# Spreading c by matmuls at the head, and the last six products in column pieces at the tail

## The chip, the core and the metric

The kernel runs on one core of one Trainium2 chip. Five engines work side by side, each through its own list of instructions in a fixed order: TensorE (PE, matmuls), VectorE (DVE), ScalarE (ACT), GpSimd (POOL) and SyncE (SP), which issues all transfers. An engine that waits for another holds up everything behind it in its own list. The metric is the device time of one execution in microseconds; the time before is the median of three runs.

## The reference

One decoder block for 1024 positions of width 1024 in float32. All six shifts, scales and gates, and the two of the last norm, come from one vector c:

```python
c_act = jax.nn.silu(c)
cond = c_act @ ada_w[i] + ada_b[i]
shift1, scale1, gate1, shift2, scale2, gate2 = jnp.split(cond, N_MOD, axis=-1)
h = modulate(rmsnorm(x, norm1_g[i]), shift1, scale1)
z = h @ w_in[i] + b_in[i]
...
x = x + gate1[:, None, :] * (y @ w_out[i])
h2 = modulate(rmsnorm(x, norm2_g[i]), shift2, scale2)
g_ff, up_ff = jnp.split(h2 @ w_ffn_in[i], 2, axis=-1)
x = x + gate2[:, None, :] * ((jax.nn.silu(g_ff) * up_ff) @ w_ffn_out[i])
shift_f, scale_f = jnp.split(c_act @ ada_f_w + ada_f_b, 2, axis=-1)
return modulate(rmsnorm(x, norm_f_g), shift_f, scale_f)
```

Between `z` and `y` stand a spatial gating mixer and a convolution; the change touches neither.

## The kernel before

**Layout.** Activations are stored transposed: eight tiles x0 to x7 of 128 channels by 1024 positions, worked on in two halves of 512 positions. A product in float32 is made of three matmuls on rounded parts (high by high, low by high, high by low, `mm3`, L731 to L733). For this each weight and each activation is split: ScalarE rounds it to the high part, and VectorE or GpSimd subtracts to get the low part. One column of conditioning (128 channels of one of the eight vectors) is a product of c with 128 rows of `ada_w`: the rows are loaded as a tile of 128 by 1024, and VectorE multiplies this with `cact` (silu of c, the same row in all partitions) and sums along it (`ada_cols`, L687).

**The head.** SyncE loads c as one row (L639), the eight tiles of the first half of x (L645), the small columns (L647), and then for k = 0 to 7 the two conditioning columns scale and shift (into the four `ypad` buffers) and the weights `wk`. TensorE copies c to all partitions by a matmul with ones (L661), and ScalarE applies Silu to it. The sums of squares for the first norm are matmuls with ones into 32 rows each (`rstd`, L780; the squares have five buffers, so the sixth waits for the first of these groups); then come the root (L783), the reciprocal (L784) and a broadcast back to 128 partitions (L786), and ScalarE copies the result to `r1a` (L792). Fourteen matmuls on ones (L669) stand where the planner puts them. For each k the tile is multiplied by the norm (L861), rounded with scale and shift by ScalarE (L863), its low part is made (L864, L865), and 24 matmuls add it into eight banks.

**The tail.** The last FFN projection is done by seven products per pair of tiles and halves, as in Strassen's scheme; products 5 and 3 end in the second half of the positions. In its last round, for n = 0 to 3, each product goes through L1063 and is added to x by VectorE (L1413). The final norm is made in pieces: half 0, and two pieces of 256 positions (`pieces`). Squares come from ScalarE (L1340) and are added by GpSimd (L1345) or go one by one to the sums (`to_partitions`, L1332); `norm` makes root, reciprocal and broadcast (L1361 to L1364), `output` multiplies (VectorE L1380, or GpSimd L1376), shifts (ScalarE L1382, L1377) and stores each tile (L1383). Of the last products only (3, 3) is cut in two pieces, and both of its pieces' norms follow it.

**What sets the order.** The code records all instructions; at its end `fix_order` plans the order of each engine's list from a table of durations (`duration`, `Clock`) and pins it. `issue_after` adds an edge that keeps one instruction behind another on the same engine.

## Time and profile before

| | us |
|---|---|
| median of three runs | 984.29 (983.1 to 984.59) |
| the profiled execution | 982.54 |
| its span | 980.7 |
| TensorE busy | 962.7 |
| first product starts | 18.22 |
| last product ends | 964.4 |
| last store issued | 978.3 |

The profile is of one execution of its own, and its times are counted from the start of the span. TensorE's busy time holds overlapping ends of matmuls; what tells where the time goes is the chain of waits, followed back from the last instruction, and the timeline of a stretch. A line of the timeline holds start, length, engine, source line, operation, tiles, and in brackets the idle time ahead of it with what ended it.

### The profile page before, as it was taken

Reading aid. Unit: us, or ns where it says so; the run is one execution under the profiler, and the core shown is the slowest. Engines: PE = TensorE matmul, PEld = TensorE weight load, DVE = VectorE, ACT = ScalarE, POOL = GpSimd, SP = SyncE. Lnnn points to the kernel's source line nnn. Section 1 sums busy time; section 2 is a strip of 40 time slices with the busy share of each in tenths; the row PEclk is TensorE's granted clock in tenths of the full one; section 3 lists DMA queues with packets and bytes.
Section 4 is the critical chain, followed back from the end, with each engine's and each line's share of the span. In section 5 each row is a group of like instructions: output and inputs, shape, how many; then the busy total and the mean of one; then the engine's idle time right before and its main releaser. Section 6 shows DMA issues by size and latency. Waiting matters only on the chain.

```text
span 980.7 us, 13307 instructions
## 1 busy us (share of the span) xinstructions
PE 962.7 (98%) x4673; PEld 778.2 (79%) x4673; DVE 852.3 (87%) x1200; ACT 474.8 (48%) x748; POOL 393.7 (40%) x232
## 2 busy tenths in 40 slices
PE   9999999999999999999999999999999999999994
PEld 5888777788878778888888888888888888888873
DVE  5999989999999563899999999989979989879946
ACT  6788566733563652564333233333338337236416
POOL 0068888646454312663454444454542100000221
PEclk9999999999999999999999999999999999999997
DMA  8982442433565334864777667665659838224104
GB/s 329 337 321 75 153 170 83 154 108 135 161 230 183 134 104 163 279 213 140 250 237 255 220 229 257 239 225 187 250 188 320 287 111 266 97 67 149 33 1 172
DMA packets 73668, 184.10 MB, mean 188 GB/s; under 512 B 8193, under 2 KB 10497, under 8 KB 73602
## 3 DMA queue, kind: packets, MB, share of 16 engines
q1 hardware_dynamic: 73602, 183.25, 54.5%
q8 instruction: 37, 0.61, 0.2%
q14 instruction: 29, 0.24, 0.1%
HBM read 142.06 MB, written 41.16 MB: 187 GB/s over the span
## 4 chain that ended last, share of the span: by engine, by line
PE 93%; ACT 2%; DVE 2%; DMA 1%; issue 1%; SPq 0%; ACTq 0%; DVEq 0%
PE B L1063 30%; PE C L1063 18%; PE ah L1063 10%; PE A L1063 3%; PE po L733 3%; PE po L731 3%; PE po L732 3%; PE p L731 3%; PE p L732 3%; PE p L733 3%; PE v L733 2%; PE pu L731 2%; PE v L731 2%; PE pu L733 2%; PE v L732 1%; PE pu L732 1%
## 5 line engine op out<-in xcount | busy, mean ns | idle before, releaser
L1063 PE MATMUL B<-h,w_f 128*128 128x512 f32 x816 | 191.0, 389 | 0.1
L1063 PEld LDWEIGHTS B<-h,w_f 128*128 128x128 f32 x816 | 153.0, 188 | 32.4 <-DVE w_f L1056 0.7
L1001 DVE SCALAR_TENSOR_TENSOR cv<-ypad,colt,cv 128x512 f32<-128x512 f32 x216 | 147.7, 747 | 0.2
L1063 PE MATMUL B<-fa,w_d 128*128 128x512 f32 x528 | 125.6, 389 | 0.0
L1063 PE MATMUL C<-h,w_f 128*128 128x512 f32 x528 | 124.9, 389 | 0.0
L1063 PEld LDWEIGHTS B<-fa,w_d 128*128 128x128 f32 x528 | 99.0, 188 | 20.8 <-issue 0.2
L1063 PEld LDWEIGHTS C<-h,w_f 128*128 128x128 f32 x528 | 99.1, 188 | 20.5
L1063 PE MATMUL ah<-h,wh_a 128*128 128x512 f32 x320 | 101.4, 394 | 0.5 <-ACT sg L805 0.5
L1055 ACT ACTIVATE w_f<-raw_f 128x512 fp32r<-128x512 f32 x68 | 42.4, 629 | 92.1 <-PE B L1063 40.0
L1345 POOL TENSOR_TENSOR sq_nf<-sq_nf,sq_nf 128x512 f32<-128x512 f32 x9 | 11.8, 1315 | 178.9 <-ACT sq_nf L1340 178.9
L1055 ACT ACTIVATE w_d<-raw_d 128x512 fp32r<-128x512 f32 (+1 forms) x72 | 41.7, 593 | 85.7 <-PE B L1063 38.7
L715 POOL TENSOR_TENSOR wl_a<-raw_a,wh_a 128x1024 fp32r<-128x1024 f32 x20 | 49.4, 2469 | 79.0 <-ACT wh_a L714 79.0
L1063 PEld LDWEIGHTS ah<-h,wh_a 128*128 128x128 f32 x320 | 60.1, 188 | 15.3 <-issue 1.8
L1056 DVE TENSOR_TENSOR w_f<-raw_f,w_f 128x512 fp32r<-128x512 f32 x68 | 69.0, 1023 | 2.7 <-ACT w_f L1055 2.5
L1309 POOL TENSOR_TENSOR x<-x,u 128x512 f32<-128x512 f32 x22 | 35.9, 1631 | 70.8 <-DVE u L1308 58.2
L1063 PE MATMUL C<-fa,w_d 128*128 128x512 f32 (+1 forms) x273 | 64.3, 384 | 0.0
L1063 PE MATMUL ah<-h,wl_a 128*128 128x512 f32 x160 | 62.6, 392 | 0.0
L1063 PEld LDWEIGHTS C<-fa,w_d 128*128 128x128 f32 x273 | 49.9, 188 | 10.8 <-issue 1.0
L1413 DVE SCALAR_TENSOR_TENSOR x<-B,cond,x 128x512 f32<-128x512 f32 x48 | 35.9, 748 | 19.6 <-PE B L1063 19.4
L1056 DVE TENSOR_TENSOR fa<-a,fa 128x512 fp32r<-128x512 f32 x77 | 51.1, 707 | 0.5 <-ACT fa L1055 0.5
L1056 DVE TENSOR_TENSOR w_d<-raw_d,w_d 128x512 fp32r<-128x512 f32 (+1 forms) x72 | 49.4, 693 | 0.6 <-ACT w_d L1055 0.6
L1055 ACT ACTIVATE fa<-a 128x512 fp32r<-128x512 f32 x77 | 46.8, 628 | 6.4 <-DMA a<-acts 3.2
(240 smaller groups left out, 2104.1 us busy)
## 6 DMA issues: line engine op xcount, KB each, us to landing
acts<-x SPq DMA_DIRECT2D x77, 256.0 KB, 3.0
a<-acts SPq DMA_DIRECT2D x77, 256.0 KB, 4.2
raw_f<-wf SPq DMA_DIRECT2D x32, 512.0 KB, 4.6
ada<-ada SPq DMA_DIRECT2D x24, 512.0 KB, 4.3
x<-ada SPq DMA_DIRECT2D x24, 512.0 KB, 4.7
raw_a<-wf SPq DMA_DIRECT2D x20, 512.0 KB, 3.6
ahead<-ahead SPq DMA_DIRECT2D x40, 256.0 KB, 2.3
ypad<-ada SPq DMA_DIRECT2D x16, 512.0 KB, 6.1
```

Source lines behind the costliest of these rows:

```text
L715: lo_eng.tensor_tensor(lo, raw, hi.bitcast(F32), op=ALU.subtract)
L731: PE.matmul(acc, shi, mhi, start=start, stop=False)
L732: PE.matmul(acc, slo, mhi, start=False, stop=False)
L733: PE.matmul(acc, shi, mlo, start=False, stop=stop)
L1001: V.scalar_tensor_tensor(accs[j], src, wc, accs[j], op0=ALU.mult, op1=ALU.add)
L1055: A.activation(dst[:, 0, :], src, AF.Copy)
L1056: lo_eng.tensor_tensor(dst[:, 1, :], src, dst[:, 0, :].bitcast(F32), op=ALU.subtract)
L1063: last_mm = PE.matmul(bank[:, cols], s, m[:, cols], start=first and p == 0 and i == 0, stop=p == n - 1 and i == 2, skip_group_check=True)
L1309: G.tensor_tensor(g1, g1, u2, op=ALU.mult)
L1345: G.tensor_tensor(sums[half], sums[half], t, op=ALU.add)
L1413: V.scalar_tensor_tensor(xs[k][:, part], bank[:, cols], ccol(GATE2, k), xs[k][:, part], op0=ALU.mult, op1=ALU.add)
```

## The change

*c.* It is loaded as eight columns, 128 partitions by 8, into the tile `cond`. ScalarE applies Silu to these 8 columns (`cvec`). Eight matmuls spread each column over all partitions: the column, repeated 128 times, is the stationary side and an identity the moving one. GpSimd makes the identity (`ident`) by a fill and an `affine_select`. ScalarE copies the two banks to `cact`. The table for the root is loaded behind the one Silu.

*The first column of scale.* Its weights come in another layout (`ada0`) and are contracted by eight matmuls of one column each with `cvec`; VectorE finishes scale and shift of k = 0. The other columns are made as before.

*The first tile.* VectorE multiplies it by the norm from the bank itself and rounds it with scale and shift (`tensor_scalar`); the copy `r1a` comes behind that. Its 24 matmuls stand in three rows of eight.

*The ones-matmuls.* Five, four and three of 128 columns stand at fixed places: ahead of the first sums, ahead of the broadcast, ahead of the first product. The sums of squares and the broadcast are pinned in that order.

*The tail.* Products (1..3, 5) and (1..3, 3) are each made in two pieces of 256 columns, all six for piece 1 first and then all six for piece 2, and each piece has its own squares, sums and norm. A bank of sums is used by blocks of 64 columns in four row groups. Outputs of pieces 1 and 2 are stored two tiles at a time.

*The planner's table* gets a floor of 0.2 for narrow float32 matmuls, another transfer rate for the first 20 us and edges between readers of one PSUM bank on different engines.

The core of the diff:

```diff
-N_WARM = 14
+WARM = (5, 4, 3, 4)
...
+FIRST_RATES = ((9.5, 300e3), (20.0, 410e3))
...
-            t = {128: 0.219, 32: 0.068}.get(m, 0.109 if k > 64 else 0.055) * n / 128
+            t = max({128: 0.219, 32: 0.068}.get(m, 0.109 if k > 64 else 0.055) * n / 128, 0.2 if n < 32 else 0.0)
...
+                            if written or wrote or (o.space == "PSUM" and other.engine != s.engine):
...
-    c_row = sb.tile([P, D], F32, tag="raw", name="c_row", bufs=N_RAW)
-    c_load = nc.sync.dma_start(c_row[0:1, :], c).ins
+    cond = const.tile([P, 64], F32, name="cond")
+    c_load = nc.sync.dma_start(cond[:, 0:KD], c).ins
...
+    ident = sb.tile([P, D], F32, tag="raw", name="ident", bufs=N_RAW)[:, 0:P]
+    G.memset(ident, 1.0)
+    G.affine_select(out=ident, in_=ident, compare_op=ALU.is_equal, fill=0.0, base=0,
+                    pattern=[[1, P]], channel_multiplier=-1)
+    cvec = const.tile([P, KD], F32, name="cvec")
+    silu = A.activation(cvec, cond[:, 0:KD], AF.Silu).ins
+    warm = const.tile([P, 1], F32, name="warm")
+    with issue_after(silu):
+        sqrt_table = A.activation(warm, epst, AF.Sqrt).ins
     cact = const.tile([P, D], F32, name="cact")
     for h in range(2):
         cb = cv_bank(f"c{h}")
-        c_mm = PE.matmul(cb, ones[0:1].broadcast_to([1, P]), c_row[0:1, hs(h)], start=True, stop=True).ins
-        silu = A.activation(cact[:, hs(h)], cb, AF.Silu).ins
-    warm = const.tile([P, 1], F32, name="warm")
-    with issue_after(silu):
-        sqrt_table = A.activation(warm, epst, AF.Sqrt).ins
+        for j in range(4):
+            pe_last = PE.matmul(cb[:, j * P:(j + 1) * P], cvec[:, 4 * h + j:4 * h + j + 1].broadcast_to([P, P]),
+                                ident, start=True, stop=True).ins
+        with issue_after(sqrt_table):
+            A.activation(cact[:, hs(h)], cb, AF.Copy)
...
-    with issue_after(c_mm):
...
+    def keep_warm(count, ins):
+
+        for i in range(count):
+            with issue_after(ins):
+                ins = PE.matmul(warm_bank[:, 0:P], ones.broadcast_to([P, P]), ones.broadcast_to([P, P]),
+                                start=True, stop=True).ins
+        return ins
...
+    pe_last = keep_warm(WARM[0], pe_last)
...
-                PE.matmul(acc[q * 32:(q + 1) * 32], ones.broadcast_to([P, 32]), run[:, q * P:(q + 1) * P],
-                          start=g == 0, stop=g == len(groups) - 1)
+                with issue_after(pe) if pe else nullcontext():
+                    ssq = PE.matmul(acc[q * 32:(q + 1) * 32], ones.broadcast_to([P, 32]), run[:, q * P:(q + 1) * P],
+                                    start=g == 0, stop=g == len(groups) - 1).ins
+        if pe:
+            pe = keep_warm(WARM[1], ssq)
...
-            last["rstd"] = PE.matmul(
-                bank[:, q * P:(q + 1) * P], col("sel_tok", q)[rows].broadcast_to([nq * 32, P]),
-                rt, start=True, stop=True).ins
-        if not copy:
...
-        r = front.tile([P, H], F32, tag="s", name=f"r_{name}", bufs=4)
...
-        return bank[:, 0:size], r
+            with issue_after(pe) if pe else nullcontext():
+                last["rstd"] = PE.matmul(
+                    bank[:, q * P:(q + 1) * P], col("sel_tok", q)[rows].broadcast_to([nq * 32, P]),
+                    rt, start=True, stop=True).ins
...
-    r1a_bank, r1a = rstd(x_half(0), D, "n1_0", (1,) * 8, None, True, table=sqrt_table, by_dve=(3, 4, 5))
+    r1a_bank = rstd(x_half(0), D, "n1_0", (1,) * 8, None, table=sqrt_table, by_dve=(3, 4, 5), pe=pe_last)
+    r1a = front.tile([P, H], F32, tag="s", name="r_n1_0", bufs=4)
+    ada0_bank = mm_bank("ada0")
...
             with issue_after(head_loads[-1]):
-                ada_cols(m * 8 + k, dst=ypad[(2 * k + g) % 4][:, HALO:HALO + D])
+                if k == g == 0:
+                    first = sb.tile([P, D], F32, tag="raw", name="ada_first", bufs=N_RAW)
+                    ada_dma[m * 8] = nc.sync.dma_start(first, ada0)
+                    for j in range(KD):
+                        PE.matmul(ada0_bank[:, 0:1], unit_cols(first, j), cvec[:, j:j + 1],
+                                  start=j == 0, stop=j == KD - 1)
+                else:
+                    ada_cols(m * 8 + k, dst=ypad[(2 * k + g) % 4][:, HALO:HALO + D])
...
+        h = h1[0][k] = act_tile(f"h1_0_{k}", 0)
+        if k == 0:
+            V.tensor_scalar(ccol(SCALE1, 0), ada0_bank[:, 0:1], col("norm1_g", 0), gain[:, 0:1],
+                            op0=ALU.mult, op1=ALU.add)
+            V.tensor_tensor(ccol(SHIFT1, 0), ccol(SHIFT1, 0), bcol(SHIFT1, 0), op=ALU.add)
+            t = tmp("t_h1_0_0")
+            V.tensor_tensor(t, xs[0][:, hs(0)], r1a_bank, op=ALU.mult)
+            V.tensor_scalar(h[:, 0, :], t, ccol(SCALE1, 0), ccol(SHIFT1, 0), op0=ALU.mult, op1=ALU.add)
+            A.activation(r1a, r1a_bank, AF.Copy)
+            A.activation(t, t, AF.Identity, bias=ccol(SHIFT1, 0), scale=ccol(SCALE1, 0))
+            V.tensor_tensor(h[:, 1, :], t, h[:, 0, :].bitcast(F32), op=ALU.subtract)
+            pe_last = keep_warm(WARM[2], last["rstd"])
+            for n, (w, part) in enumerate(((0, 0), (1, 0), (0, 1))):
+                for j in range(4):
+                    for vg in range(2):
+                        with issue_after(pe_last):
+                            PE.matmul(acc[j, vg], unit(w_k, 4 * vg + j)[w], h[:, part, :], start=n == 0, stop=False)
+            continue
...
-        V.tensor_tensor(t, xs[k][:, hs(0)], r1a_bank if k == 0 else r1a, op=ALU.mult)
-        h = h1[0][k] = act_tile(f"h1_0_{k}", 0)
+        V.tensor_tensor(t, xs[k][:, hs(0)], r1a, op=ALU.mult)
...
     def to_partitions(i, t):
...
-        part = cols or (slice(0, H) if half == 0 else slice(H, S))
...
+        w = blocks[i]
+        for q in range(4):
+            PE.matmul(norm_banks[i][q * 32:(q + 1) * 32, 0:w], ones.broadcast_to([P, 32]),
+                      t[:, q * w:(q + 1) * w], start=i not in begun_sums, stop=False, skip_group_check=True)
+        begun_sums.add(i)
...
     def norm(i):
-        bank, part = norm_banks[i], pieces[i]
...
+        bank, w = norm_banks[i], blocks[i]
+        rt = sb.tile([P, P], F32, tag="rt", name=f"rt_nf{i}", bufs=2)[:, 0:w]
+        A.activation(rt, bank[:, 0:w], AF.Sqrt, bias=epst, scale=1.0 / D)
         V.reciprocal(rt, rt)
-        for q in range(nq):
-            PE.matmul(bank[:, q * P:(q + 1) * P], col("sel_tok", q)[rows].broadcast_to([nq * 32, P]),
+        for q in range(4):
+            PE.matmul(bank[:, q * w:(q + 1) * w], col("sel_tok", q).broadcast_to([P, P]),
                       rt, start=True, stop=True)
...
+    def output(i, groups, by_pool=(), copy_at=1, add_by_pool=False):
+        bank, part, size = norm_banks[i], pieces[i], 4 * blocks[i]
+        for g, ks in enumerate(groups):
...
+            nc.sync.dma_start(out[ks[0]:ks[0] + len(ks), :, part].rearrange("k p s -> p k s"), t)
...
-            if m == 5:
-                c_banks[n] = cv_bank(f"C{r}_{n}")
+            if m == 5 and n not in c_banks:
+                c_banks[n] = (gn_bank if last_round and n == 3 else cv_bank)(f"C{r}_{n}")
...
         for n, m in ((0, 1), (0, 5), (0, 6), (0, 2), (0, 7), (1, 1), (0, 4), (0, 3), (1, 6), (1, 2), (1, 7),
-                     (2, 1), (1, 4), (2, 2), (2, 6), (3, 1), (2, 7), (3, 2), (3, 6), (2, 4), (1, 5), (3, 7),
-                     (2, 5), (3, 4)):
+                     (2, 1), (1, 4), (2, 2), (2, 6), (3, 1), (2, 7), (3, 2), (3, 6), (2, 4), (3, 7), (3, 4)):
...
     with issue_after(last_ins):
-        step(1, 3)
-        square(1, 1)
         norm(0)
-        step(2, 3)
...
-        output(0, (0, 1, 2, 4), by_pool=())
...
-    with tc.high_priority():
-        norm(1)
-        norm(2)
-    output(0, (3, 5, 6, 7), by_pool=(3, 5))
-    output(1)
-    output(2)
+        output(0, [(k,) for k in range(KD)], by_pool=(2, 5))
+        for i in (1, 2):
+            cols = slice(pieces[i].start - H, pieces[i].stop - H)
+            spare(i)
+            for n in (1, 2, 3):
+                step(n, 5, cols)
+            norm_banks[i] = (gn_bank, mm_bank)[i - 1](f"ssq_nf{i}")
+            early[i] = add_squares(i, (5, 6, 7), early[i])
+            to_partitions(i, early[i])
+            step(1, 3, cols)
+            step(2, 3, cols)
+            to_partitions(i, add_squares(i, (1, 2)))
+            step(3, 3, cols)
+            to_partitions(i, square(3, i))
+            with tc.high_priority():
+                norm(i)
+        output(1, [(k, k + 1) for k in range(0, KD, 2)])
+        output(2, [(k, k + 1) for k in range(0, KD, 2)])
...
-        c=arr(c),
+        c=arr(c).reshape(KD, P).T,
+        ada0=arr(ada_w)[0][:, SCALE1 * D:SCALE1 * D + P].reshape(KD, P, P).transpose(1, 0, 2).reshape(P, D),
```

What the change does to the lists of the engines is seen best at three places. At the start of GpSimd's list, before (`ypad` are the column buffers, `wl_u` is the first low part that it makes):

```order
L1547 UNCONDITIONAL_BRANCH
L801 MEMSET ypad_121 128x30
L801 MEMSET ypad_122 128x30
L801 MEMSET ypad_123 128x30
L801 MEMSET ypad_124 128x30
L715 ISA
L715 TENSOR_TENSOR wl_u_601<-raw_u_598,wh_u_600 128x1024
```

and now:

```order
L1603 UNCONDITIONAL_BRANCH
L663 MEMSET ident 128x128
L817 MEMSET ypad_122 128x30
L664 ISA
L664 AFFINE_SELECT ident<-ident 128x128
L817 MEMSET ypad_123 128x30
L817 MEMSET ypad_124 128x30
L817 MEMSET ypad_125 128x30
L731 TENSOR_TENSOR wl_u_618<-raw_u_615,wh_u_617 128x1024
```

The row ISA, which the build puts there, stood behind all fills and ahead of the first subtraction; it now stands ahead of the selection that makes the identity.

At the start of TensorE's list, before (`c` are the banks of the spread c, `ssq` the sums of squares, `sq` the squares of one tile):

```order
L661 MATMUL c_97<-c_row,ones 128x512
L661 MATMUL c_100<-c_row,ones 128x512
L669 MATMUL warm<-ones 128x256
L780 MATMUL ssq_n_0_134<-sq_n_0_0_135,ones 32x128
L669 MATMUL warm<-ones 128x256
L780 MATMUL ssq_n_0_134<-sq_n_0_0_135,ones 32x128 x3
```

and now, up to the first column by matmuls (`ada`) and the broadcast of the norm:

```order
L675 MATMUL c_104<-ident,cvec 128x128 x2
L675 MATMUL c_110<-ident,cvec 128x128 x4
L685 MATMUL warm<-ones 128x128 x5
L797 MATMUL ssq_n_0_135<-sq_n_0_0_136,ones 32x128 x4
L797 MATMUL ssq_n_0_135<-sq_n_0_1_142,ones 32x128 x4
L675 MATMUL c_104<-ident,cvec 128x128
...
L675 MATMUL c_104<-ident,cvec 128x128
L797 MATMUL ssq_n_0_135<-sq_n_0_7_178,ones 32x128 x4
L685 MATMUL warm<-ones 128x128 x4
L879 MATMUL ada_196<-cvec,ada_first 128x1 x4
L806 MATMUL ssq_n_0_135<-rt_n_0_188,colt 128x128 x4
```

The first six matmuls now read the identity, and all sums of squares stand behind them and behind five ones-matmuls.

Near the end of VectorE's list, before (`C2_3` is the bank of product 5 or 3 of n = 3, `of0`, `of1`, `of2` the outputs of half 0, piece 1 and piece 2):

```order
L1413 SCALAR_TENSOR_TENSOR x3_78<-C2_3_8215,cond_120,x3_78 128x256
L1380 SCALAR_TENSOR_TENSOR of0_4_8244<-x4_79,cond_120,ssq_nf0_8010 128x512
L1413 SCALAR_TENSOR_TENSOR x3_78<-C2_3_8215,cond_120,x3_78 128x256
L1362 RECIPROCAL rt_nf1_8276<-rt_nf1_8276 64x128
L1362 RECIPROCAL rt_nf2_8281<-rt_nf2_8281 64x128
L1380 SCALAR_TENSOR_TENSOR of0_6_8296<-x6_81,cond_120,ssq_nf0_8010 128x512
L1380 SCALAR_TENSOR_TENSOR of0_7_8300<-x7_82,cond_120,ssq_nf0_8010 128x512
L1380 SCALAR_TENSOR_TENSOR of1_0_8304<-x0_75,cond_120,ssq_nf1_8203 128x256
```

and now:

```order
L1465 SCALAR_TENSOR_TENSOR x1_76<-C2_1_8210,cond_72,x1_76 128x256
L1411 RECIPROCAL rt_nf1_8296<-rt_nf1_8296 128x64
L1465 SCALAR_TENSOR_TENSOR x2_77<-C2_2_8221,cond_72,x2_77 128x256
L1465 SCALAR_TENSOR_TENSOR x3_78<-C2_3_8232,cond_72,x3_78 128x256
L1432 SCALAR_TENSOR_TENSOR of1_0_8395<-x0_75,cond_72,ssq_nf1_8243 128x256
```

Piece 1's reciprocal moved ahead of the last two additions to x, and no output of half 0 stands behind the last addition any more.

More of the change, by code (lines that the diff above doesn't have):

```diff
@@ L357, in run @@
             begin = max(t + self.wait + (LOAD_WAIT if s.load else STORE_WAIT), self.queue + gap)
-            self.queue = begin + s.bytes / (LOAD_RATE if s.load else STORE_RATE)
+            rate = LOAD_RATE if s.load else STORE_RATE
+            if self.throttled:
+                rate = next((r for until, r in FIRST_RATES if begin < until), rate)
+            self.queue = begin + s.bytes / rate
             self.last = s.load
@@ L587, in block_kernel @@
 @with_exitstack
-def block_kernel(ctx: ExitStack, tc: tile.TileContext, xT, c, ada, cols, vbias, bs, wsp,
+def block_kernel(ctx: ExitStack, tc: tile.TileContext, xT, c, ada0, ada, cols, vbias, bs, wsp,
                  wv, wu, wk, wvg, wo, wf, wfo, wfl, cst, out):
@@ L757, in modulated, with rstd @@
         return h
-    def rstd(srcs, n, name, groups, add_eng, copy=False, size=H, tmp=tmp, bank=None, table=None, by_dve=()):
+    def rstd(srcs, n, name, groups, add_eng, size=H, tmp=tmp, bank=None, table=None, by_dve=(), pe=None):
         bank = (bank or nrm_bank)(f"ssq_{name}")
@@ L867, in block_kernel @@
             for vg in range(2):
-                mm3(acc[j, vg], unit(w_k, 4 * vg + j), full(h), k == 0, k == KD - 1)
+                mm3(acc[j, vg], unit(w_k, 4 * vg + j), full(h), False, k == KD - 1)
     first_phase_loaded = ada_dma[SHIFT1 * 8 + KD - 1].ins
@@ L1351, in early_sums @@
-    def early_sums(half):
-        for i, p in enumerate(pieces):
-            if (p.start >= H) == (half == 1):
-                to_partitions(i, sums[half][:, p.start - half * H:p.stop - half * H])
-    def norm(i):
-        bank, part = norm_banks[i], pieces[i]
-        nq = (part.stop - part.start) // P
-        rows = slice(0, nq * 32)
-        rt = sb.tile([P, P], F32, tag="rt", name=f"rt_nf{i}", bufs=2)[rows]
-        A.activation(rt, bank[rows, 0:P], AF.Sqrt, bias=epst[rows], scale=1.0 / D)
+    blocks = [P, 64, 64]
@@ new lines, in block_kernel, with piece, square, spare @@
+    norm_banks, begun_sums = {}, set()
+    def piece(k, i):
+        return xs[k][:, pieces[i]]
+    spare_squares = {}
+    def square(k, i):
+        size = 4 * blocks[i]
+        free = spare_squares.get(i)
+        t = free.pop(0) if free else ev(f"sq_nf{i}_{k}")[:, 0:size]
+        A.activation(t, piece(k, i), AF.Square)
+        return t
+    def spare(i):
+        size = 4 * blocks[i]
+        wide = [sb.tile([P, D], F32, tag="raw", name=f"sqs_nf{i}_{n}", bufs=N_RAW) for n in range(2)]
+        spare_squares[i] = [w[:, q * size:(q + 1) * size] for w in wide for q in range(4)]
@@ new lines, in to_partitions, with add_squares @@
+    def to_partitions(i, t):
+        w = blocks[i]
[3 more added lines that the diff above has]
+        begun_sums.add(i)
+    def add_squares(i, tiles, run=None):
+        for k in tiles:
+            t = square(k, i)
+            if run is None:
+                run = t
+            else:
+                G.tensor_tensor(run, run, t, op=ALU.add)
+        return run
```

85 lines of the change are left out of this document (29 added, 56 removed).

## The prediction

> **What bounds the kernel now.** I read the page first: the busy times and the shares of the chain that ended last.
>
> ```profile
> PE 962.7 (98%) x4673; PEld 778.2 (79%) x4673; DVE 852.3 (87%) x1200; ACT 474.8 (48%) x748; POOL 393.7 (40%) x232
> ...
> PE 93%; ACT 2%; DVE 2%; DMA 1%; issue 1%; SPq 0%; ACTq 0%; DVEq 0%
> ```
>
> TensorE is busy for 962.7 of 980.7 us and carries 93% of the chain. Between the first and the last product it hardly waits, so a microsecond saved or lost ahead of the first product moves the end by as much, and so does one behind the last. The change works at these two places; I looked at each by itself. The chain of waits, in order of time, at the head:
>
> ```profile
> 7.66 7.19 DMA raw_k<-wk
> ...
> 14.87 1.06 ACT wh_k L714
> ...
> 16.11 0.49 ACT r_n L792
> ...
> 16.63 0.70 DVE t_h L861
> ...
> 17.35 0.82 ACT h L863
> ...
> 18.22 0.50 PE p L731
> ```
>
> The first product starts at 18.22. Its weights land at 14.85 (7.66 + 7.19) and are rounded by 15.93; behind that come the copy of the norm, the multiplication and ScalarE's rounding of the first tile. The timeline of the tail:
>
> ```profile
> 963.09 1.33 PE L1063 MATMUL C<-fa,w_d 128*128 128x256 f32 x9
> ...
> 967.25 4.92 DVE L1380 SCALAR_TENSOR_TENSOR of<-x,cond,ssq_nf 128x512 f32<-128x512 f32 x11
> ...
> 969.98 6.47 ACT L1382 ACTIVATE of<-of,cond 128x256 f32<-128x256 f32 x16
> 970.53 7.81 SPq L1383 DMA_DIRECT2D out<-of  x16
> 972.39 3.01 DVE L1380 SCALAR_TENSOR_TENSOR of<-x,cond,ssq_nf 128x256 f32<-128x256 f32 x7 [0.22 <-DMA out<-of]
> ```
>
> The last product ends at 964.4, and 16.3 us of norm, output and stores follow with no product beside them. SyncE issues the last sixteen stores 0.49 us apart (7.81 / 16) and ends at 978.3; the span ends 2.4 us behind that.
>
> **The head: how late is the identity?** TensorE is in order, and its first six matmuls now spread c with the help of an identity that Pool makes. The rows for that:
>
> ```profile
> 0.80 0.29 POOL L801 MEMSET ypad<- 128x30 f32 x4 [0.29 <-POOLq L1542]
> 51.68 5.40 POOL L715 TENSOR_TENSOR wl_u<-raw_u,wh_u 128x1024 fp32r<-128x1024 f32 x2 [50.60 <-ACT wh_u L714]
> ...
> 71.66 1.10 POOL L820 TENSOR_SCALAR_AFFINE_SELECT wt<-wt 128x1024 f32<-128x1024 f32 x1
> ```
>
> ```profile
> DMA to landing us min/median/max: 2.7/5.1/6.0
> ```
>
> In the order, a row named ISA stands ahead of Pool's first operation that isn't a fill. Before, this was a subtraction at 51.68, ahead of which Pool sat idle for 50.60 us: whatever the row costs lay in that gap. Now it stands ahead of the AFFINE_SELECT that makes the identity, near 1.1. Its price is bounded by 0 and 50.6. [...] The selection is 1.10 for 1024 columns, so between 0.14 and 1.10 for 128; I take 0.3. The identity is ready at 1.1 + 7.2 + 0.3 = 8.6.
>
> [...]
>
> What follows on the path, with the prices of the rows:
>
> ```profile
> 5.98 1.22 PE L669 MATMUL warm<-ones 128*128 128x256 f32 x2
> ...
> 9.78 0.70 PE L669 MATMUL warm<-ones 128*128 128x256 f32 x2
> ...
> 10.41 1.30 PE L780 MATMUL ssq_n<-sq_n,ones 128*32 128x128 f32 x40
> ...
> 11.04 0.17 DVE L848 SCALAR_TENSOR_TENSOR gain<-colt 128x8 f32<-128x8 f32 x1 [0.73 <-DMA colt<-cols]
> ...
> 12.38 1.23 DVE L687 SCALAR_TENSOR_TENSOR ypad<-ypad,cact 128x1024 f32<-128x1024 f32 x1 [1.18 <-DMA ypad<-ada]
> ...
> 12.76 0.37 ACT L783 ACTIVATE rt_n<-ssq_n,epst 128x128 f32<-128x128 f32 x1 [1.09 <-PE ssq_n L780]
> ...
> 13.54 0.95 DVE L784 RECIPROCAL rt_n<-rt_n 128x128 f32<-128x128 f32 x1
> ...
> 14.91 1.05 PE L786 MATMUL ssq_n<-rt_n,colt 128*128 128x128 f32 x8
> ...
> 16.02 0.58 ACT L792 ACTIVATE r_n<-ssq_n 128x512 f32<-128x512 f32 x1
> ...
> 17.23 1.22 DVE L715 TENSOR_TENSOR wl_k<-raw_k,wh_k 128x1024 fp32r<-128x1024 f32 x1
> ```
>
> ```profile
> L917 DVE TENSOR_SCALAR vn<-vn,mv,sd x8: 446/1487/2608, 142.3 to 177.3; 128x512 f32<-128x512 f32 x8
> ```
>
> - The same pair of passes takes 1.22 us at 5.98 and 0.70 at 9.78: the array is slow until it has been busy for 5 to 7 us. A 128-column matmul is 1.05 / 4 = 0.26, so 0.46 slow. Six for c and five ones-matmuls: 11 x 0.46 = 5.1, to 13.7. [...]
> - Eight groups of sums of squares (20 matmuls in 1.30, so 0.26 a group) 2.1, two late c matmuls 0.5, four changes of shape at 0.2: 3.4, to 17.1. The fifth to eighth square wait for buffers that these groups free, as now.
> - ScalarE: the copy of one half of c (0.58, queued ahead of the root) and the root (0.37) end at about 17.85; reciprocal 0.95, to 18.8. The broadcast ended 1.5 behind the reciprocal before (14.49 to 15.96), so 20.3. Beside it VectorE sums the first shift column (1.23), hidden.
> - Multiplication 0.70, two one-column steps at 0.17, rounding on VectorE at 0.45 (the fastest row of its kind; the slow ones ran beside Pool, which idles here). First product at **21.85**, 3.6 later than before.
>
> In the shadow of the 8.6 lie, at no cost, the load of c in eight columns (a row of x took 2.7), its Silu, and the table load that ScalarE saves. Behind the waiting matmuls stand all sums of squares, and behind the copies of c on ScalarE the last two squares; both are in the list. The matmuls for the first column, before and behind the broadcast, end while VectorE multiplies. If that cover is gone they cost 4 x 0.26 = 1.0. The second k: behind the rounding VectorE has the low half of the weights 1.22, a column 1.23, the low half of the tile 0.69, a column 1.23 and the next multiplication 0.69, then ScalarE rounds in 0.82: 5.9. TensorE needs the tile after 24 products. These rows show them and the tile's price:
>
> ```profile
> 20.66 0.69 DVE L865 TENSOR_TENSOR h<-t_h,h 128x512 fp32r<-128x512 f32 x1
> ...
> 22.04 0.82 ACT L863 ACTIVATE h<-t_h,cond 128x512 fp32r<-128x512 f32 x1 [0.89 <-DVE t_h L861]
> ...
> 23.89 0.39 PE L731 MATMUL p<-h,wh_k 128*128 128x512 f32 x1
> ```
>
> From 18.22 to 23.66 (23.89 less a weight load) the first k took 5.4, and its successor was ready at 22.9. Now VectorE begins this run later against the first product: a stall of 0.6. Each later k takes 5.4 on TensorE against at most 5.1 on VectorE (the five prices), so it comes once. Head: 3.6 + 0.6 = **+4.2**.
>
> **The tail.** The rows:
>
> ```profile
> 950.33 2.20 PE L1063 MATMUL B<-fa,w_d 128*128 128x512 f32 x9
> ...
> 960.40 1.33 PE L1063 MATMUL C<-fa,w_d 128*128 128x256 f32 x9
> 961.66 1.50 PE L1332 MATMUL ssq_nf<-sq_nf,ones 128*32 128x128 f32 x22
> ```
>
> ```profile
> 961.01 1.98 ACT L1382 ACTIVATE of<-of,cond 128x512 f32<-128x512 f32 x3 [0.25 <-DVE of L1380]
> ...
> 962.90 0.40 ACT L1340 ACTIVATE sq_nf<-x 128x256 f32<-128x256 f32 x1
> ...
> 964.45 0.48 DVE L1413 SCALAR_TENSOR_TENSOR x<-C,cond,x 128x256 f32<-128x256 f32 x1 [1.17 <-PE C L1063]
> ...
> 965.20 0.94 DVE L1362 RECIPROCAL rt_nf<-rt_nf 64x128 f32<-64x128 f32 x1 [0.26 <-ACT rt_nf L1361]
> ...
> 966.20 0.71 PE L1364 MATMUL ssq_nf<-rt_nf,colt 64*128 64x128 f32 x4 [0.26 <-DVE rt_nf L1362]
> ```
>
> A whole product is busy for 2.20 and a half for 1.33, both with some 0.15 that overlaps what follows; five more split products cost 5 x (2 x 1.18 - 2.05) = 1.5 at most, 1.1 at least. The block of sums between the two old halves (1.43) goes, the other groups only move. I let the last product end 0.2 earlier, at 964.2 on the old scale. By then all eight tiles of half 0 are out, and piece 1 has its root: only its broadcast stands behind the last product (0.7, to 965.0; VectorE's last update, 0.48, ends before). From 965.1 VectorE writes sixteen pieces at 0.43 (3.01 / 7), with one reciprocal of 64 columns between (0.94 for 128; I take 0.55): to 972.55. ScalarE's last piece ends 0.5 later, the store is issued by 973.45, and the span ends 2.4 to 2.6 behind it, at 976.0: **-4.7**. Eight stores of two tiles replace sixteen, so SyncE's 0.49 a store is no longer the pace. In the middle only the planner's order shifts by a few rows: 0, within 0.5 either way.
>
> Sum: 4.2 - 4.7 = **-0.5 us**. The profiled execution took 982.54 (span 980.7 and 1.8 around it), 1.75 under the median of the runs; from 982.0 I add this back: **983.8**.
>
> **The rivals.**
> - *The ISA row is free* (chance 0.27). For it: no row of before shows time for it. Then c is spread by 6, and the path is bound by the weights, rounded at 15.93, and the column's own load: first product near 16.5, -1.7, with the stall 0.6: head -1.1, total -5.8, **978.5**.
> - *The identity comes later still* (0.15), the one that ends slower. Each us of it beyond 7.2 delays every step of the list; at 7.7 the head eats the tail's gain. [...] At 11 us the total is +3.3: **987.6**.
> - *The tail gains less* (0.10). Between the norm of half 0 and the last product ScalarE now has eight outputs at 0.66 to 0.8 (1.98 / 3 and more for the two of Pool's), nine squares at 0.40 and a root: 9.5 us of work in about 11. If it falls 2 us behind, piece 1's root does too: +1.5, **985.8**. Against it: nothing else is queued there.
> - My forecast has 0.48; its own range is 981.5 to 986.
>
> **How the numbers follow.** A difference under 0.2% (2.0 us) can't be told from none. Faster: 0.27, and a fifth of the forecast's 0.48 (a load shorter than about 5.7): 0.36. Slower: most of the later identity, a little of the other two: 0.17. The rest, 0.47, is the same. The range goes from 978.2, into the free row's case, to 987.4, near the late one.
>
> **What would show it.** Pool's AFFINE_SELECT starting near 8.3 and TensorE's first matmul near 8.6 show the late identity; a first matmul before 4 shows the free row. A first product at 21.9, a short wait for h at the second k and none at later ones, the last product followed by piece 1's broadcast at once and a tail of about 12 us in place of 16.3 show the other steps. I am wrong if the first product starts before 18, or if the stores behind the last product still set the pace.

## The result, and the profile after

The changed kernel takes 977.63 us (median of 4 runs, 976.81 to 978.34) against 983.69 for the kernel before beside it (982.77 to 984.59): a ratio of 0.9939, 95% interval 0.9926 to 0.9953. It is faster by 6.1 us where 0.5 was forecast, and 0.6 us below the range.

The page of the changed kernel, busy times and chain:

```profile
PE 959.4 (98%) x4766; PEld 782.4 (80%) x4766; DVE 867.0 (89%) x1206; ACT 472.4 (48%) x752; POOL 397.9 (41%) x240
PE 92%; DVE 4%; DMA 2%; ACT 1%; issue 1%; SPq 0%; DVEq 0%; ACTq 0%
```

TensorE still carries the chain. The start of GpSimd's timeline in the changed kernel answers the question on which the forecast stood:

```profile
0.80 0.20 POOL L663 MEMSET ident<- 128x128 f32 x1 [0.29 <-POOLq L1598]
0.94 0.12 POOL L817 MEMSET ypad<- 128x30 f32 x1
1.10 0.29 POOL L664 TENSOR_SCALAR_AFFINE_SELECT ident<-ident 128x128 f32<-128x128 f32 x1
```

The selection starts 0.04 us after the fill in front of it ends (0.94 + 0.12 = 1.06). The row ISA between them in the list leaves no gap. The traces do have a row for it, on GpSimd's queue (POOLq) and at its source line; the view of that line lists it by another name, with count, shortest, median and longest time in ns, and first and last start in us. Before, and now:

```profile
L715 POOLq MODIFY_POOL_CONFIG  x2: 11/11/11, 1.0 to 1.1; - x2
```

```profile
L664 POOLq MODIFY_POOL_CONFIG  x2: 11/11/11, 1.0 to 1.0; - x2
```

It takes 11 ns each time and stood at the start before the change too, not somewhere in the 50.60 us of GpSimd's gap; only a cost that no row shows could have lain there. The identity is ready at 1.39, not at 8.6, and TensorE waits for the Silu of c instead. TensorE's timeline from there to the first product:

```profile
2.79 2.90 PE L675 MATMUL c<-ident,cvec 128*128 128x128 f32 x12 [2.79 <-ACT cvec L667]
5.48 2.34 PE L685 MATMUL warm<-ones 128*128 128x128 f32 x10
...
10.17 0.42 PE L797 MATMUL ssq_n<-sq_n,ones 128*32 128x128 f32 x8 [0.26 <-DVE sq_n L786]
10.92 0.42 PE L797 MATMUL ssq_n<-sq_n,ones 128*32 128x128 f32 x8 [0.33 <-DVE sq_n L786]
11.52 0.42 PE L797 MATMUL ssq_n<-sq_n,ones 128*32 128x128 f32 x8 [0.17 <-ACT sq_n L789]
...
14.45 1.14 PE L806 MATMUL ssq_n<-rt_n,colt 128*128 128x128 f32 x8
...
17.49 2.08 PE L903 MATMUL p<-h,wh_k 128*128 128x512 f32 x8 [0.34 <-DVE h L894]
```

The sums of squares wait for squares, so the list now runs ahead of its data. What holds it is the loading of x, and then ScalarE and VectorE, in their own timelines:

```profile
10.84 1.29 ACT L789 ACTIVATE sq_n<-x 128x512 f32<-128x512 f32 x2 [3.05 <-DMA x<-xT]
...
12.40 0.60 ACT L678 ACTIVATE cact<-c 128x512 f32<-128x512 f32 x1 [0.18 <-PE c L675]
12.89 0.36 ACT L802 ACTIVATE rt_n<-ssq_n,epst 128x128 f32<-128x128 f32 x1
```

```profile
14.36 1.23 DVE L703 SCALAR_TENSOR_TENSOR ypad<-ypad,cact 128x1024 f32<-128x1024 f32 x1
...
15.63 0.69 DVE L893 TENSOR_TENSOR t_h<-x,ssq_n 128x512 f32<-128x512 f32 x1
...
16.80 0.55 DVE L894 TENSOR_SCALAR h<-t_h,cond 128x512 fp32r<-128x512 f32 x1
```

ScalarE is idle for 3.05 us until the last tiles of x land. The first product starts at 17.49 against 18.22 before. The end of the timeline of all engines:

```profile
961.70 1.57 PE L1109 MATMUL C<-fa,w_d 128*128 128x256 f32 x11
...
963.11 1.00 PE L1413 MATMUL ssq_nf<-rt_nf,colt 128*128 128x64 f32 x8
...
964.14 2.05 DVE L1432 SCALAR_TENSOR_TENSOR of<-x,cond,ssq_nf 128x256 f32<-128x256 f32 x5 [0.35 <-PE ssq_nf L1413]
...
966.11 0.54 DVE L1411 RECIPROCAL rt_nf<-rt_nf 128x64 f32<-128x64 f32 x1
...
966.71 1.41 PE L1413 MATMUL ssq_nf<-rt_nf,colt 128*128 128x64 f32 x8 [1.93 <-DVE rt_nf L1411]
...
968.16 3.22 DVE L1432 SCALAR_TENSOR_TENSOR of<-x,cond,ssq_nf 128x256 f32<-128x256 f32 x8 [0.42 <-PE ssq_nf L1413]
```

The last product ends at 963.27. Piece 1's broadcast follows at once, VectorE starts its outputs at 964.14, and the span ends at 975.1. By stages, from the two traces:

| us | before | after | difference |
|---|---|---|---|
| first product starts | 18.22 | 17.49 | -0.7 |
| first product to end of the last | 946.2 | 945.8 | -0.4 |
| behind the last product | 16.3 | 11.8 | -4.5 |
| span | 980.7 | 975.1 | -5.6 |

The tail came as forecast. The head was to cost 4.2 us and gave 0.7.

### The profile page after: what moved, and what is told of

Read it like the earlier page. It is cut to its first block, busy times and chain, and to the rows that moved or that the text cites. A ratio compares the mean times of both kernels' runs of the same rounds, so it can differ in the third digit from the quotient of the medians.

```text
span 975.1 us, 13473 instructions
## 1 busy us (share of the span) xinstructions
PE 959.4 (98%) x4766; PEld 782.4 (80%) x4766; DVE 867.0 (89%) x1206; ACT 472.4 (48%) x752; POOL 397.9 (41%) x240
## 4 chain that ended last, share of the span: by engine, by line
PE 92%; DVE 4%; DMA 2%; ACT 1%; issue 1%; SPq 0%; DVEq 0%; ACTq 0%
PE B L1109 31%; PE C L1109 19%; PE ah L1109 11%; PE A L1109 4%; PE po L747 3%; PE po L748 3%; PE po L749 3%; PE v L747 2%; PE pu L747 2%; PE v L749 2%; PE pu L748 2%; PE v L748 1%; PE pu L749 1%; PE p L747 1%; PE p L748 1%; PE p L749 1%
## 5 line engine op out<-in xcount | busy, mean ns | idle before, releaser
L1404 POOL TENSOR_TENSOR sq_nf<-sq_nf,sq_nf 128x512 f32<-128x512 f32 (+1 forms) x7 | 8.5, 1228 | 166.9 <-ACT sq_nf L1383 162.6
L1102 DVE TENSOR_TENSOR w_f<-raw_f,w_f 128x512 fp32r<-128x512 f32 x68 | 73.0, 1084 | 0.5 <-ACT w_f L1101 0.4
L1109 PEld LDWEIGHTS C<-fa,w_d 128*128 128x128 f32 x318 | 52.6, 189 | 8.8 <-issue 0.4
L1352 POOL TENSOR_TENSOR x<-x,up 128x512 f32<-128x512 f32 x20 | 32.7, 1633 | 42.2 <-ACT x L1351 42.2
```

Source lines behind the costliest of these rows:

```text
L1102: lo_eng.tensor_tensor(dst[:, 1, :], src, dst[:, 0, :].bitcast(F32), op=ALU.subtract)
L1109: last_mm = PE.matmul(bank[:, cols], s, m[:, cols], start=first and p == 0 and i == 0, stop=p == n - 1 and i == 2, skip_group_check=True)
L1352: G.tensor_tensor(g0, g0, up0, op=ALU.mult)
L1404: G.tensor_tensor(run, run, t, op=ALU.add)
```

## The experiments

All times are medians, beside runs of the kernel before on the same chip. "First" and "last" in the table are the start of the first and the end of the last product; "x" is the median and longest time from issue to landing of the eight loads of the first half of x.

| kernel | time, ratio to before (interval) | x | first | last | span |
|---|---|---|---|---|---|
| before | | 5.1, 6.0 | 18.22 | 964.42 | 980.7 |
| changed | 977.63, 0.9939 (0.9926 to 0.9953) | 6.2, 6.8 | 17.49 | 963.27 | 975.1 |
| head_only | 982.34, 0.9989 (0.998 to 0.9998) | 4.9, 6.0 | 16.70 | 963.63 | 980.5 |
| tail_only | 978.3, 0.9944 (0.9932 to 0.9957) | 6.0, 6.6 | 19.25 | 965.57 | 976.8 |
| late_ident | 982.68, 0.9989 (0.9979 to 0.9998) | 5.7, 6.3 | 22.94 | 968.99 | 980.5 |
| late_norm | 977.64, 0.9939 (0.9925 to 0.9953) | 6.2, 6.9 | 17.54 | 962.96 | 976.1 |
| after_again | 977.33, 0.9936 (0.9924 to 0.9949) | 5.3, 6.2 | 16.84 | 963.54 | 975.4 |
| one_tile_stores | 979.08, 0.9956 (0.9944 to 0.9969) | 5.9, 6.6 | 17.05 | 966.45 | 978.7 |
| early_table | 974.68, 0.9908 (0.9895 to 0.9922) | 5.1, 5.8 | 16.24 | 960.93 | 972.9 |
| all_three | 977.45, 0.9941 (0.9928 to 0.9954) | 5.0, 5.8 | 16.38 | 963.52 | 975.7 |
| late_half | 978.64, 0.9954 (0.9942 to 0.9966) | 5.4, 6.1 | 16.70 | 962.16 | 976.7 |
| early_copy | 977.24, 0.9939 (0.9926 to 0.9951) | 5.9, 6.6 | 17.18 | 963.87 | 975.9 |
| move_32 | 974.79, 0.9913 (0.9899 to 0.9926) | 5.3, 6.0 | 16.47 | 961.05 | 972.6 |
| move_32_root | 975.25, 0.9917 (0.9903 to 0.993) | 6.0, 6.7 | 17.14 | 962.53 | 974.4 |

### The two halves of the change alone: head_only, tail_only

Each has one end of the change and the old code at the other, for the first:

```diff
-        output(1, [(k, k + 1) for k in range(0, KD, 2)])
-        output(2, [(k, k + 1) for k in range(0, KD, 2)])
+    output(1)
+    output(2)
```

> The new head with the old tail. Theory A (the identity is there at 1.4 us, so the list of TensorE starts early, but its end is held by the loads of x and by VectorE): first product at 17.5 within 0.4, the tail behind the last product 16.3 as before, the time 0.7 to 1.2 us under the kernel before. Rival B (the term on record, an identity at 8.6): first product at 21.9, 4.2 us slower. Rival C (the free row of the prediction, with the path it gave): first product at 16.5, 1.1 us or more faster.

> The old head with the new tail. Theory A (head and tail add up): first product at 18.2, last product 0.2 to 0.4 us earlier than before, 11.8 us from there to the end of the span; 4.7 to 4.9 us faster. Rival B (the tail's gain comes in part with the new head, through a shifted plan): 3 us or less faster.

Measured: 1.0 us faster (982.34 against 983.37) and 5.1 us faster (978.3 against 983.37). Their sum, 6.1, is the whole change, so within their intervals the ends add up. Of the first, theory A's time holds, but its first product was too late: 16.70. Of the second, theory A's sum holds, though its profile has the first product at 19.25 and not at 18.2, and 11.2 us behind the last. The landings of x, from what the trace tells of the tile x in head_only and in tail_only, go with these first products:

```profile
DMA to landing us min/median/max: 3.2/4.9/6.0
```

```profile
DMA to landing us min/median/max: 2.8/6.0/6.6
```

In the old head, x landing after 5.1 us (median) gave a first product at 18.22, and after 6.0 at 19.25. In the new head 4.9 gave 16.70 and 6.2 gave 17.49. For like landings the new head is 1.5 to 1.8 us ahead, near the prediction's rival with the free row (16.5, 1.7 earlier). By the longest landing, which puts the first products of this head in order (6.0: 16.70; 6.2: 16.84; 6.6: 17.05; 6.8: 17.49), the lead is 1.5 at 6.0 and 2.2 at 6.6; only two profiles have the old head. The first pair of profiles compared a quick landing before with a slow one after and hid half of it.

So the first product gains 1.5, but head_only only 1.0. Its profile has 16.9 us behind the last product, 0.6 more than before, and TensorE's timeline shows a wait that neither kernel with the old head has:

```profile
61.47 0.50 PE L747 MATMUL pu<-h,wh_u 128*128 128x512 f32 x1 [0.95 <-ACT sg L821]
```

### An identity that does come late: late_ident

```diff
-    ident = sb.tile([P, D], F32, tag="raw", name="ident", bufs=N_RAW)[:, 0:P]
+    wide = sb.tile([P, D], F32, tag="raw", name="ident", bufs=N_RAW)
+    for i in range(8):
+        G.memset(wide, 1.0)
+    ident = wide[:, 0:P]
```

> The changed kernel with eight wide fills on GpSimd ahead of the identity, so that it comes several us late, near 8.6 if a fill of 1024 columns takes 0.9 us; all other lists are unchanged. Theory A (the sum on record was right but for the identity's time: every us is handed on): with the identity at t, the first product starts at t + 13.2, and the time is that much above the changed kernel less 17.5, plus a stall of 0.6. Rival B (part of the delay is slack, since the sums wait for x until 12.7 anyway): first product at t + 10.5 to t + 11.5, so 19 to 20 for t = 8.6, the time 2 to 3 us above the changed kernel.

GpSimd's timeline, and TensorE's, in this kernel:

```profile
8.86 0.20 POOL L666 MEMSET ident<- 128x128 f32 x1
9.14 0.60 POOL L667 TENSOR_SCALAR_AFFINE_SELECT ident<-ident 128x128 f32<-128x128 f32 x1
```

```profile
9.80 2.93 PE L678 MATMUL c<-ident,cvec 128*128 128x128 f32 x12 [9.80 <-POOL ident L667]
...
17.74 0.42 PE L800 MATMUL ssq_n<-sq_n,ones 128*32 128x128 f32 x8
...
19.90 1.14 PE L809 MATMUL ssq_n<-rt_n,colt 128*128 128x128 f32 x8
...
22.94 2.08 PE L906 MATMUL p<-h,wh_k 128*128 128x512 f32 x8 [0.34 <-DVE h L897]
```

The identity is ready at 9.74 and the first product starts 13.2 us later, at 22.94. The prediction had 13.25 between the two (21.85 less 8.6). On the way the sums end 8.4 behind the identity (18.16; 8.5 in the prediction) and the broadcast 11.3 (21.04; 11.7). Theory A holds to 0.1 us: the long sum over the path was right, and only the time at which it begins was wrong. That it is so close is in part luck: from the sums to the end of the broadcast the path took 2.9 where 3.2 were forecast, and from there to the first product 1.9 where it was 1.55. The time is 5.0 us above the changed kernel's. Against that kernel the first matmul is 7.0 us later and the first product 5.45: the other 1.6 were slack, since the sums wait for x. The stall of 0.6 at the second k isn't there, neither here nor in the changed kernel.

The row ISA stands here too between the fill (which ends at 9.06) and the selection at 9.14, with no more than 0.08 us between.

This kernel also tells of the wait at the sigmoids. It is there, 0.87 us at 67.63, though the first product is 4.7 us later than before the change: it doesn't come from an earlier start, but from the order of the new lists. A load of weights (`raw_u`) waits for a buffer that VectorE's product for a column (`ada`) reads (2.5 us of SyncE's waiting in the changed kernel); first in tail_only, with the old head, then here:

```profile
51.82 1.22 DVE L687 SCALAR_TENSOR_TENSOR ada<-ada,cact 128x1024 f32<-128x1024 f32 x1
...
52.71 5.40 POOL L715 TENSOR_TENSOR wl_u<-raw_u,wh_u 128x1024 fp32r<-128x1024 f32 x2 [51.63 <-ACT wh_u L714]
...
53.08 0.33 SPq L709 DMA_DIRECT2D raw_u<-wu  x1
```

```profile
55.97 5.99 POOL L734 TENSOR_TENSOR wl_u<-raw_u,wh_u 128x1024 fp32r<-128x1024 f32 x2 [46.22 <-PE p L752]
...
56.26 3.43 DVE L706 SCALAR_TENSOR_TENSOR ada<-ada,cact 128x1024 f32<-128x1024 f32 x1
...
59.73 0.33 SPq L728 DMA_DIRECT2D raw_u<-wu  x1
```

With the old head GpSimd's subtraction starts 0.9 us behind the product, which takes 1.22 us. With the new one it starts 0.3 ahead, and the product beside it takes 3.43. The load is issued 36.8 us behind the first product here and in the changed kernel, 33.8 with the old head. No run tests this by itself.

### The tail's parts: late_norm, late_half, one_tile_stores

late_norm puts both norms behind the last square, late_half four outputs of half 0 behind the last addition to x, and one_tile_stores stores each tile by itself:

```diff
-            with tc.high_priority():
-                norm(i)
+        for i in (1, 2):
+            with issue_after(last["square"]):
+                norm(i)
```

```diff
-        output(0, [(k,) for k in range(KD)], by_pool=(2, 5))
+        output(0, [(k,) for k in (0, 1, 2, 4)], by_pool=(2,))
...
+        with issue_after(last["update"]):
+            output(0, [(k,) for k in (3, 6, 5, 7)], by_pool=(5,))
```

```diff
-            nc.sync.dma_start(out[ks[0]:ks[0] + len(ks), :, part].rearrange("k p s -> p k s"), t)
+            for n, k in enumerate(ks):
+                nc.sync.dma_start(out[k, :, part], t[:, n, :])
```

> The changed kernel with the root of piece 1 behind the last square of piece 2, so that both norms follow the last product, as before the change. Theory A (having piece 1's norm ahead of the last product is worth what its chain takes less the gap that it leaves later): first output of piece 1 2.0 us later against the last product, last output and the end 1.3 us later. Rival B (the end is set by stores or by ScalarE): the end at most 0.3 us later.

> The changed kernel with four outputs of half 0 (three multiplied by VectorE, one by GpSimd) behind the last addition to x, as before the change. Theory A (taking half 0 out of the tail is the largest part of the tail's gain): VectorE has 3 x 0.67 and ScalarE 4 x 0.7 more behind the last product, the end 2.0 to 2.8 us later against the last product, and the time as much. Rival B (VectorE waits there for piece 1's norm anyway and hides them): 1.2 us or less.

> The changed kernel with sixteen stores of one tile for pieces 1 and 2 in place of eight of two tiles. Theory A (SyncE's 0.49 us a store is the pace once more, as it was before the change): from the last product to the last store 0.5 to 0.8 us longer than in the changed kernel, the end as much later. Rival B (with the norm of piece 1 early, VectorE and ScalarE at 0.41 us a piece set the pace): no difference beyond 0.3 us.

VectorE behind the last product in late_norm (which ends there at 962.96) and in late_half (962.16):

```profile
964.17 1.10 DVE L1411 RECIPROCAL rt_nf<-rt_nf 128x64 f32<-128x64 f32 x2 [0.68 <-ACT rt_nf L1410]
965.99 6.35 DVE L1432 SCALAR_TENSOR_TENSOR of<-x,cond,ssq_nf 128x256 f32<-128x256 f32 x16 [0.72 <-PE ssq_nf L1413]
```

```profile
964.04 1.41 DVE L1432 SCALAR_TENSOR_TENSOR of<-x,cond,ssq_nf 128x512 f32<-128x512 f32 x2 [0.20 <-ACT r_nf L1421]
965.36 0.55 DVE L1411 RECIPROCAL rt_nf<-rt_nf 128x64 f32<-128x64 f32 x1
965.83 6.26 DVE L1432 SCALAR_TENSOR_TENSOR of<-x,cond,ssq_nf 128x256 f32<-128x256 f32 x16
```

*late_norm.* From the last product the first output of piece 1 starts 3.0 us later (0.87 in the changed kernel), the last output ends after 9.4 (8.1) and the span after 13.1 (11.8): theory A's 1.3 in the trace. The times of the runs don't show it (977.64 against 977.63): the last product came 0.4 earlier against the first, and what is left lies within the intervals. So this part is worth about 1 us by the trace and isn't settled by the times.

*late_half.* The span ends 14.5 us behind the last product, 2.7 later, and the time is 1.4 to 1.6 us above the changed kernel's (4.7 us faster than before, against 6.1 and 6.3). That is theory A in the trace; the times lie between the two theories. A part of the 2.7 is again that the plan moved piece 1's norm back.

*one_tile_stores.* The time is 1.75 us above after_again. By the trace most of that isn't the stores: TensorE takes 2.7 us more between the first and the last product, of which 1.90 is a wait at 88.39 that came with the new plan (the profiled execution, with 980.44, was the slowest of the five). In the tail:

```profile
971.45 3.22 DVE L1432 SCALAR_TENSOR_TENSOR of<-x,cond,ssq_nf 128x256 f32<-128x256 f32 x8 [1.38 <-PE ssq_nf L1413]
```

VectorE waits 1.38 us for piece 2's norm (0.42 in the changed kernel), yet its last output ends only 0.1 us later behind the last product (8.2 against 8.1). The last store is issued 9.9 us behind the last product instead of 9.15, which is theory A's 0.5 to 0.8, but the span ends only 0.4 later, near rival B's 0.3. So the stores still count for something, and halving their number is worth 0.4 us at most.

### The changed kernel again, and the sigmoid: after_again, early_table

early_table adds one activation that nobody reads behind the last rounding of the first phase, so that the table is loaded there:

```diff
+    with issue_after(h_low):
+        A.activation(warm, epst, AF.Sigmoid)
     first_phase_loaded = ada_dma[SHIFT1 * 8 + KD - 1].ins
```

> The changed kernel once more, to be timed beside the next three. Theory A (the first product follows the loads of x, which land at other times in each execution): first product between 16.7 and 17.5 us, and 1.5 to 1.8 us ahead of what the kernel before shows for the same landing of x; the time as before, 977.6 within 0.7. Rival B (the new head itself makes x land late, by its c in eight columns): x's median landing 6.2 us again, first product 17.5.

> The changed kernel with ScalarE's table for the sigmoid loaded some 3 us earlier, by a small activation that nobody reads, placed behind the last rounding of the first phase, where ScalarE waits for weights. Theory A (the new head's plan lost 0.8 us near 62, where TensorE waits for the sigmoid behind a table load): the wait for sg goes, 0.8 us faster than the changed kernel. Rival B (something else is late there as well, the weights or VectorE): a wait of the same size with another name, no gain.

after_again has the same list as the changed kernel, and x landed in 5.3 us instead of 6.2: first product at 16.84. That is theory A; the eight columns of c don't by themselves make x late. Its span is no shorter all the same, because TensorE lost 0.9 us more between the first and the last product than in the first profile, among it 0.22 in a wait near 744; most of that wasn't traced.

ScalarE's timeline near 58 in the changed kernel, and in early_table:

```profile
57.88 1.06 ACT L730 ACTIVATE wh_u<-raw_u 128x1024 fp32r<-128x1024 f32 x1 [2.35 <-DMA raw_u<-wu]
58.96 1.28 ACT L821 ACT_TABLE_LOAD   x1
60.26 2.42 ACT L821 ACTIVATE sg<-p,colt 128x512 f32<-128x512 f32 x4
```

```profile
56.94 1.06 ACT L730 ACTIVATE wh_u<-raw_u 128x1024 fp32r<-128x1024 f32 x1 [2.17 <-PE p L748]
57.90 2.41 ACT L821 ACTIVATE sg<-p,colt 128x512 f32<-128x512 f32 x4
```

In the changed kernel the table load of 1.28 stands behind weights that land late, the four sigmoids start at 60.26, and TensorE needs a bank that they read: it waits 0.82 us for them, until 62.15. (In one_tile_stores, where the plan puts the rounding of these weights behind the four sigmoids, the wait isn't there either.) In early_table the load is out of the way, at 50.76, they start at 57.90, and the wait is gone. The kernel is 2.65 us faster than after_again, more than theory A's 0.8. By the spans (972.9 against 975.4): 0.6 at the first product, where x landed 0.2 to 0.4 earlier; 2.0 between first and last product, of which the wait near 62 is 0.7. Against the first profile of the changed kernel it is 1.1 between the products. The wait for the sigmoid is shown; the other 0.3 to 1.3, a new plan and chance together, stays open.

### Three tries to do better: all_three, early_copy, move_32 and move_32_root

all_three: early_table, and

```diff
-    r1a_bank = rstd(x_half(0), D, "n1_0", (1,) * 8, None, table=sqrt_table, by_dve=(3, 4, 5), pe=pe_last)
+    r1a_bank = rstd(x_half(0), D, "n1_0", (1,) * 8, None, table=sqrt_table, by_dve=(3, 4, 5, 7), pe=pe_last)
...
-        output(1, [(k, k + 1) for k in range(0, KD, 2)])
+        with issue_after(root):
+            output(1, [(k, k + 1) for k in range(0, KD, 2)], by_pool=(3, 5), add_by_pool=True)
```

> The early table, and two more: VectorE squares the last tile of x in the head, so that the last two squares don't follow each other on ScalarE (first product 0.4 to 0.8 us earlier for the same landing of x); and in the tail ScalarE's root of piece 2 stands ahead of its outputs and GpSimd makes two outputs of piece 1 (the gap of 0.4 us on VectorE goes, and 0.8 us of its outputs). Theory A: 1.6 to 2.4 us faster than the changed kernel. Rival B (VectorE gives back in the head what ScalarE saves, and GpSimd's two outputs end last or slow VectorE): 0.8 us, the early table alone.

early_copy puts all eight matmuls that spread c first, and the second copy of c ahead of the last squares:

```diff
-    pe_last = keep_warm(WARM[0], pe_last)
+    with issue_after(*spread):
+        pe_last = keep_warm(WARM[0], pe_last)
```

> The changed kernel with all eight matmuls that spread c ahead of the first ones-matmuls, and ScalarE's second copy of c ahead of its last two squares; the other lists are the same. Theory A (in the changed kernel this copy stands ahead of the root and holds it by 0.5 us): root, reciprocal, broadcast and the first product 0.3 to 0.5 us earlier for the same landing of x, and the time as much. Rival B (the chain waits for the loads of x and of the first weights anyway): 0.1 us or less. The wait for the sigmoid near 62 stays in both.

move_32 is early_table with `(2, 7), (3, 6), (2, 4), (3, 7), (3, 2), (3, 4)` as the last whole products, move_32_root has in addition the root of piece 2 ahead of the outputs of piece 1 (the edge of all_three, without GpSimd).

> The kernel with the early table, and product (3, 2) moved between (3, 7) and (3, 4), which use the same bank one behind the other in the changed kernel, where TensorE waits 0.6 us near 944 for VectorE's addition to x. Theory A: this wait goes, 0.5 us faster than with the early table alone. Rival B (the norm of half 0 comes later, because a square of tile 3 does, and its outputs move into the tail): 0 to 1 us slower.

> The kernel before this one, and in the tail ScalarE's root of piece 2 ahead of the outputs of piece 1. Theory A (the gap of 0.4 us on VectorE between the two pieces goes): 0.3 to 0.5 us faster than without it. Rival B (ScalarE starts its sixteen outputs later and ends as late): no difference.

*all_three* is 2.8 us slower than early_table. Its first product is no earlier than early_table's (16.38 with x at 5.0, 16.24 with 5.1), so VectorE's square bought nothing; its tail is 12.2 us; and TensorE takes 2.4 us more between the products. 0.95 of it is a wait at 958.41 for VectorE's addition to x, which early_table doesn't have there. Which of its edits brings that wasn't separated.

*early_copy* shows what holds the head now. In VectorE's timeline:

```profile
12.87 0.95 DVE L806 RECIPROCAL rt_n<-rt_n 128x128 f32<-128x128 f32 x1 [1.13 <-ACT rt_n L805]
14.32 1.23 DVE L706 SCALAR_TENSOR_TENSOR ypad<-ypad,cact 128x1024 f32<-128x1024 f32 x1 [0.49 <-DMA ypad<-ada]
```

The reciprocal starts 0.4 us earlier than in the changed kernel (13.29), but VectorE then waits for the load of the first shift column. The first product is 0.3 earlier with x landing 0.2 to 0.3 earlier, and the time is the changed kernel's (0.9939 against 0.9939 and 0.9936). Rival B: the loads hold it.

*move_32* took away the wait near 944 (0.49 at 942.69 in early_table) but its time is that of early_table (0.9913 and 0.9908), and *move_32_root* changed nothing that the runs can tell (0.9917). The best version is early_table, 2.65 us below the changed kernel beside it.

## Why the prediction was wrong

**The step that failed** is the 7.2 us for the row ISA, and with it "The identity is ready at 1.1 + 7.2 + 0.3 = 8.6". The bounds were 0 and 50.6, and the value between them was the author's estimate: the price of a row of another kind, the load of the first weights by SyncE (7.19). No run shows this term, nor the 11 us of the rival with the later identity: the row takes 11 ns, and the selection starts 0.04 us behind the fill in the changed kernel, at 1.10, and 0.08 behind it in late_ident, at 9.14. The row itself was in the trace before the change, 11 ns near 1.0 us. With all that may hang on it, it cost 0.04 us. What the row does, the runs don't tell.

**The sum behind it was right.** late_ident made the identity late and got 13.2 us from there to the first product, forecast 13.25 (its terms as written add up to 13.2). The one price in it that is not fixed is that of the eleven first matmuls, all taken at the slow 0.46. In the changed kernel six took 2.90 and five 2.34, as forecast, but the same five took less in other executions of the same list, as the timeline of late_half shows:

```profile
5.48 1.62 PE L685 MATMUL warm<-ones 128*128 128x128 f32 x10
```

A pass takes 0.23 slow and 0.15 fast (ten in 2.34 here, eight in 1.16 later), so two or three of these ten were slow: by this estimate the array became fast some 3 us after its first matmul at 2.79, in the changed kernel's profile only after 5. In late_ident, whose first matmul starts at 9.80, the same five took 2.34; in tail_only, with the old head, the pair of passes priced in the prediction still took 1.22 at 10.04, 7.6 us after the first matmul at 2.49, and 0.70 at 12.68. So the 5 to 7 us that the prediction read from the profile before are that execution's and no rule. The moment moved no first product, since the sums wait for x.

**The stall at the second k** (0.6) didn't come; TensorE's first three rows of eight took 5.6 us (17.49 to 23.05) and the second tile was ready at 22.89: the steps between took 5.6 where the forecast had 5.9, and began 0.2 ahead of the first product. A wait of 0.7 to 0.95 came in its place at the end of the phase, at the sigmoids. The prediction had "in the middle only the planner's order shifts by a few rows: 0, within 0.5", and looked for no table load there. The order of the lists changed far behind the place that was edited, and GpSimd and VectorE met at a buffer that a load waits for.

**The tail** was forecast 4.7 us shorter, with the last product 0.2 earlier; it is 4.5 behind the last product and 0.4 ahead of it in the profiles, and 5.1 in tail_only's times. The chain was as described: the broadcast of piece 1 at once, VectorE at 0.39 to 0.41 us a piece, no store setting the pace (storing each tile by itself moved the end by 0.4). ScalarE fell behind by no more than a step: its root of piece 2 stands behind two outputs, and VectorE waits 0.42 for it. By one trace each, most of the gain is half 0 being out of the way (2.7), then piece 1's early norm (1.3), and least the wider stores (0.4).

**The rivals and the range.** What happened is the rival with the free row (0.27), whose 978.5 came within 0.9 us. In that there is luck: it had the stall of 0.6, which didn't come, and not the wait of 0.7 to 0.95, which did. Its path was another too. It had the weights and the load of a column hold the first product; in the changed kernel the weights are rounded by 16.59 and the tile only by 17.35, the first product follows the landing of x, and a wait for the column's load shows only in later kernels such as early_copy. (The rival of the smaller tail is 985.3 by its own terms, 983.8 + 1.5, and not 985.8.) The range ended at 978.2, 0.3 below that rival's value, as if its own terms had no error. The terms did: 16.5 for the first product (16.7 and 16.8 with x landing early, 17.5 late), 5.8 in all (6.1 measured). With a rival at more than a quarter, the range should have taken in that rival's own spread, at least the 0.8 us by which the first product varies.

## What to carry to other kernels

An entry in an engine's list that the timeline doesn't show is first looked for in the other views: here that of its source line had it. Where only a cost behind it is in question, ask what else would show it, and if nothing does, let nothing and a full price be two cases of equal standing, each with its own spread. Before comparing the start of two executions, set them side by side at the same landing of their loads; here one profile of each showed 0.7 us of a gain of 1.5. And when a planner orders the lists anew, look for the waits that it brings far from the edit: here a table load of 1.28 us behind weights that land late brought a wait of 0.7 to 0.95, about half of the head's gain of 1.5, and one idle activation in the right place took that wait away.
